# Memory attention: values with the weight as the moving operand, keys with both memory parts in one pass, and an 8-column product in two passes

## The chip, the cores and the metric

One core of a Trainium2 chip runs the whole program. The metric is the device time of one execution in microseconds (us); shorter is better. The engines are TensorE (PE in the profile; its weight loads are PEld), VectorE (DVE), ScalarE (ACT), GpSimd (POOL) and SyncE (SP, which issues nearly all transfers).

## What is computed

The reference runs two transformer blocks in float32 on 512 tokens of 1024 channels. The second block has a gated delta-rule mixer, an attention from the 512 tokens to 256 memory tokens, and a feed-forward part. What the change touches, in the reference's own words:

```python
proj = hn @ w_in[l]                                   # 2568 columns; the last 8 are b (4) and a (4)
beta = jax.nn.sigmoid(b)
g = -jnp.exp(a_log) * jax.nn.softplus(a + dt_bias)
...
m = rmsnorm_2(mem, mem_norm_g[l])                     # 256 x 1024
q = (h @ w_q).reshape(B, S, 4, 256)                   # 512 tokens
k = (m @ w_k).reshape(B, M, 4, 256)                   # 256 memory tokens
v = (m @ w_v).reshape(B, M, 4, 256)
s = jnp.einsum('bshd,bmhd->bhsm', q, k) * 256 ** -0.5
o = jnp.einsum('bhsm,bmhd->bshd', jax.nn.softmax(s, axis=-1), v).reshape(B, S, D_MODEL)
return o @ w_o
```

## The kernel before

Activations lie transposed: 8 chunks of 128 channels (partitions) by 512 tokens. Every large product is taken in a reduced float32 format (fp32r) with each operand split into a high part (a ScalarE cast) and a low part (the rest, one VectorE subtraction). `mm3` (line 224) makes three matmuls from a pair of blocks: high x high, high x low, low x high. A `unit` (line 230) takes one weight tile of 128 partitions x 1024 elements, that is 8 blocks of 128 x 128, and makes 128 output channels with 8 x 3 matmuls into one PSUM bank; the weight is the stationary operand and the activations are the moving one, 512 columns, or 256 for the memory. The result is evacuated by VectorE and ScalarE with the norm's factor, then split again. A `group` (line 247) starts several units with their first `part` chunks and finishes the rest afterwards, so that TensorE has work while the last chunks of the input come in.

Weights come in the order of a plan (`unit_plan`, line 65) written out by hand. `w_dma` (line 165) loads a tile of 512 KB on SP's queue into one of two staging buffers "wst"; `w_split` (line 175) makes its high part "wh" on ScalarE (L187) and its low part "wl" on VectorE (L188), three buffers each. `w_prefetch` (line 191) splits up to two tiles and loads up to four ahead of the unit.

TensorE executes in the order of the program. The other engines' instructions are ordered when the program is built, by a priority: the place in the program, with evacuations, splits and loads of a unit raised by 400 places (`high_priority`). Background work is written as generators in a list; `tick` (line 206) lets each take one step after a unit, and so TensorE's instructions of such a step stand between two units.

The second mixer (`mix2`, line 1165) begins with a group of two units with `part` 6: the tile with the 8 gate columns (number 20 of `w_in_2`, the columns 0 to 3 and 32 to 35 of an otherwise empty tile) and unit 0. `gates` (line 864) transposes the gate rows and computes the decay on VectorE (L875 to L895); two small matmuls (L899, L900) use it. At its end the output projection runs 8 units of 4 blocks (`w_out_21`, line 1235), with `mem_prep` (line 1288) in the background: it loads the memory, splits it with its gain, sums its squares on GpSimd, and in its fifth step makes the norm of the memory's 256 tokens (`norm_R`, line 347: a matmul with ones into the PSUM tile "sm", which has one buffer at this point, then Ln, Exp and a correction step, L298 to L305).

The memory attention (`xa`, line 1315) runs the units of `XA_ORDER` (line 56): keys 0 to 2, then for each head two query units with keys between, then two value units. Keys and values are made transposed, 24 matmuls of 256 columns each. A value unit's result is scaled and, one tick later, turned by two transposes (L1331) and split into "xv". `xhead` (line 1246) is a head's attention in four steps: the scores of the 512 tokens and their softmax; an empty step; the transposes of the probabilities and their split; the product with the values, which overwrites the head's queries in "oh" and "ol". The output projection follows as a group of three units and five single units.

Of the kernel before, what the change touches and what calls it, by code (L numbers as in the profile page):

```python
# [9 lines left out]
F32 = mybir.dt.float32  # L10
F32R = mybir.dt.float32r
# [4 lines left out]
P = 128  # L16
S = 512
D = 1024
# [34 lines left out]

XA_ORDER = [("w_xk_2", m) for m in range(3)]
for _h in range(4):
    for _m in (2 * _h, 2 * _h + 1):
        XA_ORDER.append(("w_xq_2", _m))
        if 3 + _m < 8:  # L60
            XA_ORDER.append(("w_xk_2", 3 + _m))
    XA_ORDER += [("w_xv_2", 2 * _h), ("w_xv_2", 2 * _h + 1)]


def unit_plan():
# [40 lines left out]
class Kern:  # L106
# [68 lines left out]
    def w_split(self, i, parts=1):  # L175
        if i >= len(self.plan) or i in self.split_:
            return
        self.w_dma(i)
        nb = self.plan[i][2]
        st = self.staged[i]  # L180
        h = self.pw.tile([P, nb * P], F32R, tag="wh", name=self.nm("wh"), bufs=3)
        l = self.pw.tile([P, nb * P], F32R, tag="wl", name=self.nm("wl"), bufs=3)
        self.split_[i] = (h, l)
        n = nb * P // parts
        for p in range(parts):
            c = slice(p * n, p * n + n)
            r = self.nc.scalar.copy(h[:, c], st[:, c])  # L187
            self.nc.vector.tensor_tensor(out=l[:, c], in0=st[:, c], in1=h[:, c].bitcast(F32), op=ALU.subtract)  # L188
        return r
# [32 lines left out]


    def mm3(self, ps, h, l, xh, xl, first, last):
        mm = self.nc.tensor.matmul
        self.last_mm = mm(ps, h, xh, start=first, stop=False)  # L226
        mm(ps, h, xl, start=False, stop=False)  # L227
        mm(ps, l, xh, start=False, stop=last)  # L228

    def unit(self, name, idx, xs, evac, N=S, fill=0, mid=None, ps=None):  # L230
# [16 lines left out]
    def group(self, entries, xs, part, drain=False, fill=0):  # L247

        begun = []
        for i, (name, m, evac) in enumerate(entries):  # L250
            self.mark(f"{name}/{m}")
            wh, wl = self.w_get(name, m)
            ps = self.mm()
            begun.append((wh, wl, ps, evac))
            for k in range(part):
                sl = slice(k * P, k * P + P)
                self.mm3(ps[:], wh[:, sl], wl[:, sl], *xs[k], k == 0, False)
                if k == 0 and fill:
                    self.take(fill, self.last_mm)
            with self.tc.high_priority(offset=self.BOOST):  # L260
                self.w_prefetch(max(1, min(self.AHEAD_SPLIT, 2 - i)))
            if drain:
                self.tick()
        if drain:
            self.drain()
        for wh, wl, ps, evac in begun:
            for k in range(part, len(xs)):
                sl = slice(k * P, k * P + P)
                self.mm3(ps[:], wh[:, sl], wl[:, sl], *xs[k], False, k == len(xs) - 1)
            with self.tc.high_priority(offset=self.BOOST):  # L270
                self.w_prefetch()
                evac(ps)
            if not drain:
                self.tick()
# [589 lines left out]
    def gates(self, bar):  # L864
        nc = self.nc
        v, tt = nc.vector, nc.vector.tensor_tensor
        yield
        yield
        ps = self.sm()
        for n in range(4):  # L870
            nc.tensor.transpose(ps[:, n * P:(n + 1) * P], bar[:, n * P:(n + 1) * P], self.ccol("ident"))
        pv = ps[:].rearrange("p (n c) -> p n c", n=4)
        v4 = lambda t: t[:].rearrange("p (n h) -> p n h", n=4)
        beta, y, w, e, s2, p = (self.small(k) for k in ("beta", "gy", "gw", "ge", "gs2", "gp"))
        v.tensor_scalar(out=v4(beta), in0=pv[:, :, 0:4], scalar1=-1.0, scalar2=80.0, op0=ALU.mult, op1=ALU.min)  # L875
        tt(out=v4(y), in0=pv[:, :, 32:36], in1=self.vcol("dt_bias_2", 0, 16).rearrange("p (n h) -> p n h", n=4),
           op=ALU.add)
        v.scalar_tensor_tensor(out=w[:], in0=y[:], scalar=-1.0, in1=y[:], op0=ALU.mult, op1=ALU.max)
        nc.scalar.activation(e[:], w[:], AF.Exp, scale=-1.0)
        nc.scalar.activation(beta[:], beta[:], AF.Exp)  # L880
        v.tensor_scalar(out=beta[:], in0=beta[:], scalar1=1.0, scalar2=None, op0=ALU.add)
        v.reciprocal(beta[:], beta[:])
        v.tensor_scalar(out=w[:], in0=e[:], scalar1=2.0, scalar2=None, op0=ALU.add)
        v.reciprocal(w[:], w[:])
        tt(out=e[:], in0=e[:], in1=w[:], op=ALU.mult)
        tt(out=s2[:], in0=e[:], in1=e[:], op=ALU.mult)
        v.tensor_scalar(out=p[:], in0=s2[:], scalar1=1.0 / 17, scalar2=None, op0=ALU.mult)
# [12 lines left out]
        nc.tensor.matmul(ps[:, 16:32], self.ccol("gt"), g[:], start=True, stop=True)  # L900
        bg, kd = self.small("gbg"), self.small("gkd")
        nc.scalar.activation(bg[:], ps[:, 0:16], AF.Exp)
        nc.scalar.activation(kd[:], ps[:, 16:32], AF.Exp)
        tt(out=bg[:], in0=bg[:], in1=beta[:], op=ALU.mult)
        self.g_beta, self.g_g, self.g_bg, self.g_kd = beta, g, bg, kd
        self.g_last = self.small("glast")
# [381 lines left out]
    def mem_prep(self):  # L1288

        nc = self.nc  # L1290
        M = 256
        mem = self.big("mem", F32R)[:].rearrange("p c (h t) -> p h c t", h=2)
        macc, raw = self.pm.tile([P, M], F32, tag="msum", name="msum"), []
        for i in range(4):
            raw.append(self.c5("memr", 4)[:, :S].rearrange("p (k t) -> p k t", k=2))
# [1 line left out]
        for k in range(ND):  # L1297
# [6 lines left out]
                self.split(mem[:, 0, k, :], mem[:, 1, k, :], src, self.vcol("mem_norm_g_2", k))  # L1304
            if k % 2 == 1:
                yield
        ops = [(mem[:, 0, k, :], mem[:, 1, k, :]) for k in range(ND)]
        for _ in range(0):
            yield
        self.mem = ops, self.norm_R([macc[:]], N=M, after=self.last_sq)  # L1310

    last_mm = None
    mem = None
# [1 line left out]
    def xa(self, gnext):  # L1315
# [5 lines left out]
        if self.mem is None:  # L1321
            self.bg.append(self.mem_prep())
            self.drain()
        ms, RM = self.mem
        self.xk = self.pm.tile([P, 2, 8, M], F32R, tag="xk", name="xk")
        self.xv = self.pm.tile([P, 2, 2, D], F32R, tag="xv", name="xv")
        def v_tr(m, t):
            yield
            ps = self.pd()
            for mb in range(2):  # L1330
                nc.tensor.transpose(ps[:, mb * P:mb * P + P], t[:, mb * P:mb * P + P], self.ccol("ident"))  # L1331
            self.split(self.xv[:, 0, :, m * P:m * P + P], self.xv[:, 1, :, m * P:m * P + P],
                       ps[:, :M].rearrange("p (a c) -> p a c", a=2))
        getR = self.lazy_R(xacc)
        self.oh, self.ol = self.big("oh", F32R), self.big("ol", F32R)
        for name, m in XA_ORDER:
            def ev_k(ps):
                t = self.scaled(ps, RM, N=M)
                self.split(self.xk[:, 0, m, :], self.xk[:, 1, m, :], t[:, :M])

            def ev_q(ps):
                t = self.scaled(ps, getR())
                self.split(self.oh[:, m, :], self.ol[:, m, :], t[:])

            def ev_v(ps):
                self.bg.append(v_tr(m, self.scaled(ps, RM, N=M)))
            if name == "w_xq_2":
                self.unit(name, m, xs, ev_q)
            else:
                self.unit(name, m, ms, ev_k if name == "w_xk_2" else ev_v, N=M)  # L1350
            if name == "w_xv_2" and m % 2 == 0:
                self.bg.append(self.xhead(m // 2))
        self.reload_x()
        os_ = [(self.oh[:, k, :], self.ol[:, k, :]) for k in range(ND)]
        self.units("w_xo_2", ND, os_, self.FIRST_XO, 6,
# [152 lines left out]
def layout(inp):  # L1508
# [5 lines left out]
    for t in ("ffn1", "ffn2"):  # L1514
        a[t + "_wgu"] = tile_w(g[t + "_wgu"][0])
        for s, (lo, hi) in enumerate(((0, 8), (8, 16), (16, 22))):
            a[f"{t}_wdown{s}"] = tile_w(g[t + "_wdown"][0], lo * P, hi * P)
    for n in ("w_in", "attn_proj", "conv_proj", "w_out", "ple_proj", "ple_gate_w", "w_xk_2", "w_xv_2",
              "w_xq_2", "w_xo_2", "w_up_2"):
        a[n] = tile_w(g[n][0])  # L1520
    w = g["w_in_2"][0]
    pad = np.zeros((D, 21 * P), w.dtype)
    pad[:, :2560] = w[:, :2560]
# [41 lines left out]
```

## Time and profile before

| | |
|---|---|
| median of 3 runs | 2045.68 us (2045.57 to 2047.61) |
| the profiled execution | 2047.42 us |
| its span in the profile | 2045.6 us, 25091 instructions |
| TensorE busy | 2004.0 us (98%), 9564 matmuls |
| VectorE / ScalarE / GpSimd busy | 1218.2 / 881.0 / 237.5 us |
| mean granted TensorE clock | 0.994 of full speed |

The span runs from the first instruction to the last; the profiled execution's own time has 1.8 us more around it. A matmul's end in the profile is modelled, and consecutive matmuls overlap, so the price of one is read from start to start. In brackets behind an instruction stand the idle time of its engine before it and what ended that. Transfers and semaphore waits don't count as busy.

### The profile page before, as it was taken

How to read it: one execution, taken by the hardware profiler on the slowest of the kernel's cores; microseconds unless marked ns; L12 is line 12 of the kernel's file. 1: busy time of each engine (PE TensorE's matmuls, PEld its weight loads, DVE VectorE, ACT ScalarE, POOL GpSimd, SP SyncE). 2: the span in 40 equal slices, each digit the busy share in tenths (PEclk: the TensorE clock that was granted, in tenths of full speed). 3: DMA queues.
4: the chain of work that ended last, by engine and by line, in shares of the span. 5: the costliest groups of instructions: out<-in, count | busy, mean ns of one | idle time of the engine just before them, and what ended most of it. 6: DMA issues, size and time to landing. Idle time of an engine off the chain costs nothing. (4 is left out here: it accounts for less than half of the span.)

```text
span 2045.6 us, 25091 instructions
## 1 busy us (share of the span) xinstructions
PE 2004.0 (98%) x9564; PEld 1672.0 (82%) x9564; DVE 1218.2 (60%) x1956; ACT 881.0 (43%) x1467; POOL 237.5 (12%) x234
## 2 busy tenths in 40 slices
PE   8999999999998999999999999999999999999997
PEld 6888888787887888888888877888989888888886
DVE  6434445899889865543444577677576654344344
ACT  5223223665778544422222364463464444233233
POOL 0000000296224300000000012135000000000001
PEclk9999999999899999999999999999999999999999
DMA  5232323322221234232232234221044422232322
GB/s 181 94 103 93 102 94 105 127 93 95 69 72 60 68 124 154 93 100 96 96 100 93 85 101 137 93 78 53 17 155 129 139 83 93 94 102 93 100 96 73
DMA packets 65672, 201.13 MB, mean 98 GB/s; under 512 B 7312, under 2 KB 11536, under 8 KB 65424
## 3 DMA queue, kind: packets, MB, share of 16 engines
q1 hardware_dynamic: 64864, 199.00, 29.8%
q8 instruction: 76, 1.25, 0.2%
q10 hardware_dynamic: 688, 0.53, 0.1%
q14 instruction: 44, 0.36, 0.1%
HBM read 188.75 MB, written 10.49 MB: 97 GB/s over the span
## 5 line engine op out<-in xcount | busy, mean ns | idle before, releaser
L187 ACT CAST wh<-wst 128x1024 fp32r<-128x1024 f32 (+3 forms) x357 | 353.9, 993 | 892.4 <-PE mm L227 633.8
L226 PE MATMUL mm<-xh,wh 128*128 128x512 f32 x1272 | 502.6, 395 | 2.6 <-ACT xh L290 1.5
L228 PE MATMUL mm<-xh,wl 128*128 128x512 f32 x1272 | 496.1, 390 | 0.7 <-DVE wl L188 0.5
L227 PE MATMUL mm<-xl,wh 128*128 128x512 f32 x1272 | 495.5, 390 | 0.3 <-DVE xl L291 0.3
L188 DVE TENSOR_TENSOR wl<-wst,wh 128x1024 fp32r<-128x1024 f32 (+3 forms) x357 | 420.0, 1178 | 74.3 <-ACT wh L187 73.9
L226 PEld LDWEIGHTS mm<-xh,wh 128*128 128x128 f32 x1272 | 239.1, 188 | 55.4 <-issue 3.2
L227 PEld LDWEIGHTS mm<-xl,wh 128*128 128x128 f32 x1272 | 239.1, 188 | 52.7 <-issue 3.4
L228 PEld LDWEIGHTS mm<-xh,wl 128*128 128x128 f32 x1272 | 238.9, 188 | 51.4 <-DVE wl L188 1.5
L227 PE MATMUL mm<-hl,wh 128*128 128x512 f32 (+1 forms) x616 | 238.2, 387 | 0.2
L226 PE MATMUL mm<-hh,wh 128*128 128x512 f32 (+1 forms) x616 | 238.3, 387 | 0.0
L228 PE MATMUL mm<-hh,wl 128*128 128x512 f32 (+1 forms) x616 | 238.0, 386 | 0.0
L371 DVE SCALAR_TENSOR_TENSOR x<-mm,x 128x512 f32<-128x512 f32 x111 | 76.6, 690 | 249.7 <-PE mm L228 246.9
L651 POOL TENSOR_TENSOR y<-y,cv 128x512 f32<-128x512 f32 x90 | 131.8, 1464 | 126.0 <-ACT cv L650 109.1
L227 PEld LDWEIGHTS mm<-hl,wh 128*128 128x128 f32 x616 | 115.7, 188 | 24.3 <-DVE hl L288 1.0
L226 PEld LDWEIGHTS mm<-hh,wh 128*128 128x128 f32 x616 | 115.7, 188 | 23.6
L228 PEld LDWEIGHTS mm<-hh,wl 128*128 128x128 f32 x616 | 115.7, 188 | 23.3
L226 PE MATMUL mm<-xnh,wh 128*128 128x512 f32 x304 | 121.3, 399 | 0.7 <-DVE z L389 0.7
L228 PE MATMUL mm<-xnh,wl 128*128 128x512 f32 x304 | 119.6, 394 | 0.0
L227 PE MATMUL mm<-xnl,wh 128*128 128x512 f32 x304 | 119.5, 393 | 0.0
L438 DVE TENSOR_TENSOR t<-mm,R 128x512 f32<-128x512 f32 x43 | 29.7, 691 | 138.4 <-PE mm L228 138.3
L659 DVE SCALAR_TENSOR_TENSOR cacc<-u,vec,cacc 128x512 f32<-128x512 f32 x145 | 108.9, 751 | 2.8
L432 DVE TENSOR_TENSOR t<-mm,R 128x512 f32<-128x512 f32 x43 | 29.7, 691 | 94.1 <-PE mm L228 94.0
(406 smaller groups left out, 2829.0 us busy)
## 6 DMA issues: line engine op xcount, KB each, us to landing
wst<-ffn_wgu SPq DMA_DIRECT2D x86, 512.0 KB, 3.4
wst<-w_in SPq DMA_DIRECT2D x63, 512.0 KB, 3.4
wst<-ffn_wdown SPq DMA_DIRECT2D x32, 512.0 KB, 3.4
wst<-w_up SPq DMA_DIRECT2D x32, 512.0 KB, 3.4
wst<-w_down SPq DMA_DIRECT2D x32, 512.0 KB, 3.5
wst<-ffn_wdown SPq DMA_DIRECT2D x16, 384.0 KB, 3.0
xd<-x SPq DMA_DIRECT2D x24, 256.0 KB, 2.1
x<-xd SPq DMA_DIRECT2D x24, 256.0 KB, 5.2
```

The source lines that it names most:

```text
L187: r = self.nc.scalar.copy(h[:, c], st[:, c])
L188: self.nc.vector.tensor_tensor(out=l[:, c], in0=st[:, c], in1=h[:, c].bitcast(F32), op=ALU.subtract)
L226: self.last_mm = mm(ps, h, xh, start=first, stop=False)
L227: mm(ps, h, xl, start=False, stop=False)
L228: mm(ps, l, xh, start=False, stop=last)
L371: self.nc.vector.scalar_tensor_tensor(out=x, in0=ps[:], scalar=scale, in1=x, op0=ALU.mult, op1=ALU.add)
L432: nc.vector.tensor_tensor(out=t[:], in0=ps[:], in1=R[:], op=ALU.mult)
L438: nc.vector.tensor_tensor(out=t[:], in0=ps[:], in1=R[:], op=ALU.mult)
L651: eng.tensor_tensor(out=y, in0=y, in1=t[:], op=ALU.add)
L659: yield eng.scalar_tensor_tensor(out=y if j == 29 else acc, in0=u[:, j:j + S], scalar=w(j), in1=acc, op0=ALU.mult, op1=ALU.add)
```

## The change

- **Values.** The weight `w_xv_2` is laid out by rows: tile k holds rows 128 k to 128 k + 127 with all 1024 columns, 512 KB as before. A value unit now takes chunk k of the normalised memory as the stationary operand (two blocks of 128 tokens) and the weight tile as the moving one (two halves of 512 columns), 4 x 3 matmuls of 512 columns, into four PSUM banks ("pd") that collect all eight units. The result has the memory tokens on partitions, as "xv" wants it, so the transposes are gone; the norm's factor is now one per partition.
- **That factor** is made in `mem_prep`: two matmuls of one column into "sm", one VectorE operation that reads them, and a small reciprocal root; the norm over the columns for the keys (`norm_R`) follows it.
- **Keys.** The memory's high and low parts lie side by side (2 x 256 columns), and the high weight takes both in one matmul of 512 columns; the low weight takes the high part in one of 256. The evacuation adds the two halves: a ScalarE copy and a VectorE addition are new.
- **Order.** All eight value units come first, then keys 0 and 1, then queries and keys in turn; a head's attention is appended after its second query unit.
- **The 8 gate columns.** The weight tile keeps its high part in columns 0 to 63 and its low part in 64 to 127 of one stationary tile, so that `mm3` makes two matmuls, not three; `gates` adds the two parts after its transposes.

```diff
-XA_ORDER = [("w_xk_2", m) for m in range(3)]
-for _h in range(4):
-    for _m in (2 * _h, 2 * _h + 1):
-        XA_ORDER.append(("w_xq_2", _m))
-        if 3 + _m < 8:
-            XA_ORDER.append(("w_xk_2", 3 + _m))
-    XA_ORDER += [("w_xv_2", 2 * _h), ("w_xv_2", 2 * _h + 1)]
+XA_ORDER = [("w_xv_2", m) for m in range(8)] + [("w_xk_2", m) for m in range(2)]
+for _m, _k in enumerate((2, 3, 4, 5, None, 6, None, 7)):
+    XA_ORDER.append(("w_xq_2", _m))
+    if _k:
+        XA_ORDER.append(("w_xk_2", _k))
+NARROW = ("w_in_2", 20)
...
     def w_split(self, i, parts=1):
         h = self.pw.tile([P, nb * P], F32R, tag="wh", name=self.nm("wh"), bufs=3)
+        if self.plan[i][:2] == NARROW:
+            h3, s3 = (t[:].rearrange("p (k c) -> p k c", c=P) for t in (h, st))
+            r = self.nc.scalar.copy(h3[:, :, :64], s3[:, :, :64])
+            self.nc.vector.tensor_tensor(out=h3[:, :, 64:], in0=s3[:, :, :64], in1=h3[:, :, :64].bitcast(F32),
+                                         op=ALU.subtract)
+            self.split_[i] = (h, None)
+            return r
...
     def mm3(self, ps, h, l, xh, xl, first, last):
         self.last_mm = mm(ps, h, xh, start=first, stop=False)
-        mm(ps, h, xl, start=False, stop=False)
+        mm(ps, h, xl, start=False, stop=last and l is None)
+        if l is None:
+            return
         mm(ps, l, xh, start=False, stop=last)
...
     def gates(self, bar):
-        v.tensor_scalar(out=v4(beta), in0=pv[:, :, 0:4], scalar1=-1.0, scalar2=80.0, op0=ALU.mult, op1=ALU.min)
-        tt(out=v4(y), in0=pv[:, :, 32:36], in1=self.vcol("dt_bias_2", 0, 16).rearrange("p (n h) -> p n h", n=4),
-           op=ALU.add)
+        nc.scalar.copy(v4(w), pv[:, :, 64:68])
+        nc.scalar.copy(v4(e), pv[:, :, 96:100])
+        tt(out=v4(beta), in0=pv[:, :, 0:4], in1=v4(w), op=ALU.add)
+        tt(out=v4(y), in0=pv[:, :, 32:36], in1=v4(e), op=ALU.add)
+        v.tensor_scalar(out=beta[:], in0=beta[:], scalar1=-1.0, scalar2=80.0, op0=ALU.mult, op1=ALU.min)
+        tt(out=y[:], in0=y[:], in1=self.vcol("dt_bias_2", 0, 16), op=ALU.add)
...
     def mem_prep(self):
-        ops = [(mem[:, 0, k, :], mem[:, 1, k, :]) for k in range(ND)]
-        self.mem = ops, self.norm_R([macc[:]], N=M, after=self.last_sq)
+        ps, v = self.sm(), self.small("mv", 2)
+        rc = self.pt.tile([P, 2], F32, tag="rmc", name="rmc")
+        for mb in range(2):
+            nc.tensor.matmul(ps[:, mb:mb + 1], macc[:, mb * P:mb * P + P], self.ccol("ones", 0, 1),
+                             start=True, stop=True)
+        nc.vector.tensor_scalar(out=v[:], in0=ps[:, :2], scalar1=1.0 / D, scalar2=EPS, op0=ALU.mult, op1=ALU.add)
+        self.rsqrt_small(v[:], rc[:], "mr")
+        self.mem = both, self.norm_R([macc[:]], N=M, after=self.last_sq), rc
...
     def xa(self, gnext):
+        def v_unit(k):
+            wh, wl = self.w_get("w_xv_2", k)
+            for i in range(4):
+                mb, cs = i // 2, slice(i % 2 * H, i % 2 * H + H)
+                ts = slice(mb * P, mb * P + P)
+                self.mm3(vps[i][:], mem[:, 0, k, ts], mem[:, 1, k, ts], wh[:, cs], wl[:, cs], k == 0, k == ND - 1)
+            with self.tc.high_priority(offset=self.BOOST):
+                self.w_prefetch()
+                if k == ND - 1:
+                    for i in range(4):
+                        at = slice(None), i // 2, slice(i % 2 * H, i % 2 * H + H)
+                        self.split(self.xv[:, 0][at], self.xv[:, 1][at], vps[i][:], RMc[:, i // 2:i // 2 + 1])
+            self.tick()
+        def k_unit(m):
+            wh, wl = self.w_get("w_xk_2", m)
+            ps = self.mm()
+            for k in range(ND):
+                sl = slice(k * P, k * P + P)
+                nc.tensor.matmul(ps[:], wh[:, sl], both[:, k, :], start=k == 0, stop=False)
+                nc.tensor.matmul(ps[:, :M], wl[:, sl], mem[:, 0, k, :], start=False, stop=k == ND - 1)
+            with self.tc.high_priority(offset=self.BOOST):
+                self.w_prefetch()
+                t = self.t2("z")
+                nc.scalar.copy(t[:, M:], ps[:, M:])
+                nc.vector.tensor_tensor(out=t[:, :M], in0=ps[:, :M], in1=t[:, M:], op=ALU.add)
+                nc.vector.tensor_tensor(out=t[:, :M], in0=t[:, :M], in1=RM[:, :M], op=ALU.mult)
+                self.split(self.xk[:, 0, m, :], self.xk[:, 1, m, :], t[:, :M])
+            self.tick()
+        vps = [self.pd() for _ in range(4)]
...
-            if name == "w_xv_2" and m % 2 == 0:
-                self.bg.append(self.xhead(m // 2))
+            if name == "w_xv_2":
+                v_unit(m)
+            elif name == "w_xk_2":
+                k_unit(m)
+            else:
+                self.unit(name, m, xs, ev_q)
+                if m % 2:
+                    self.bg.append(self.xhead(m // 2))
...
+    a["w_xv_2"] = np.ascontiguousarray(g["w_xv_2"][0].reshape(ND, P, D))
```

## Rows read from the trace of the kernel before

**Rows 1.** The page's busy time, share of the span and instructions by engine

```profile
PE 2004.0 (98%) x9564; PEld 1672.0 (82%) x9564; DVE 1218.2 (60%) x1956; ACT 881.0 (43%) x1467; POOL 237.5 (12%) x234
```

**Rows 2.** Timeline of TensorE, 1503 to 1521 us: start, duration, line, operands (us)

```profile
1503.58 0.39 PE L226 MATMUL mm<-yd,wh 128*128 128x512 f32 x1
...
1508.79 0.39 PE L228 MATMUL mm<-yd,wl 128*128 128x512 f32 x1
...
1518.00 0.28 PE L226 MATMUL mm<-mem,wh 128*128 128x256 f32 x1
...
1520.64 0.28 PE L227 MATMUL mm<-mem,wh 128*128 128x256 f32 x1
```

**Rows 3.** Timeline of TensorE at a pair of value transposes

```profile
1551.06 0.38 PE L1331 MATMUL pd<-cst,z 128*128 128x128 f32 x2
1551.19 0.36 PE L226 MATMUL pd<-xk,oh 128*128 128x256 f32 x1
1551.39 0.28 PE L227 MATMUL pd<-xk,oh 128*128 128x256 f32 x1
```

**Rows 4.** Timeline of TensorE at the start of the second mixer

```profile
1258.25 0.50 PE L226 MATMUL mm<-xh,wh 128*128 128x512 f32 x1 [1.48 <-ACT xh L290]
...
1259.38 0.63 PE L228 MATMUL mm<-xh,wl 128*128 128x512 f32 x1
1259.81 1.91 PE L350 MATMUL sm<-ss,cst 128*128 128x512 f32 x2
```

**Rows 5.** Busy time by stretch; after the five engines the granted clock, DMA share, GB/s

```profile
1258.20:1260.00 1.80, 1.47 (x4) 1.00 (x5) 0.78 (x2) 1.62 (x2) 0.00 (x0) 0.82 0.89 246
1260.00:1262.50 2.50, 2.50 (x6) 1.27 (x5) 1.22 (x1) 1.39 (x2) 0.00 (x0) 0.50 0.37 141
```

**Rows 6.** Timeline of VectorE, the gate chain

```profile
1272.49 0.16 DVE L876 TENSOR_TENSOR gy<-sm,vec 128x16 f32<-128x16 f32 x1
...
1279.25 1.01 DVE L895 SCALAR_TENSOR_TENSOR gg<-gy,ge 128x16 f32<-128x16 f32 x1
```

**Rows 7.** Timeline of TensorE, the small matmuls of the gates

```profile
1281.24 0.29 PE L899 MATMUL sm<-gg,cst 128*128 128x16 f32 x2
...
1281.61 1.10 PE L1162 MATMUL pd<-pp,wpool 128*128 128x512 f32 x2
```

**Rows 8.** Timeline of TensorE, the start of the memory attention

```profile
1521.59 0.39 PE L228 MATMUL mm<-mem,wl 128*128 128x256 f32 x1 [0.67 <-DVE wl L188]
...
1527.52 0.40 PE L227 MATMUL mm<-xl,wh 128*128 128x512 f32 x1
1528.07 0.50 PE L228 MATMUL mm<-xh,wl 128*128 128x512 f32 x1
```

**Rows 9.** Timeline of TensorE, the memory's norm

```profile
1509.02 0.59 PE L350 MATMUL sm<-msum,cst 128*128 128x256 f32 x2
```

**Rows 10.** Timeline of VectorE behind the memory's norm

```profile
1509.72 0.68 DVE L188 TENSOR_TENSOR wl<-wst,wh 128x512 fp32r<-128x512 f32 x1
...
1513.67 0.69 DVE L188 TENSOR_TENSOR wl<-wst,wh 128x512 fp32r<-128x512 f32 x1
...
1514.87 0.41 DVE L301 TENSOR_SCALAR rv<-sm 128x256 f32<-128x256 f32 x1
```

**Rows 11.** Timeline of VectorE, low parts of three weight tiles

```profile
1516.33 1.23 DVE L188 TENSOR_TENSOR wl<-wst,wh 128x1024 fp32r<-128x1024 f32 x1 [0.45 <-ACT wh L187]
...
1520.32 1.22 DVE L188 TENSOR_TENSOR wl<-wst,wh 128x1024 fp32r<-128x1024 f32 x1
...
1539.29 1.22 DVE L188 TENSOR_TENSOR wl<-wst,wh 128x1024 fp32r<-128x1024 f32 x1 [0.66 <-ACT wh L187]
```

**Rows 12.** Timeline of VectorE, evacuation of a query unit

```profile
1559.82 0.69 DVE L389 TENSOR_TENSOR z<-mm,R 128x512 f32<-128x512 f32 x1 [1.72 <-PE mm L228]
...
1561.86 0.68 DVE L288 TENSOR_TENSOR ol<-z,oh 128x512 fp32r<-128x512 f32 x1
```

**Rows 13.** Busy time by stretch, in the scans of the second mixer

```profile
1400.00:1440.00 40.00, 39.77 (x364) 39.56 (x365) 22.92 (x88) 17.27 (x59) 10.67 (x22) 1.00 0.03 8
```

More of the change, by code (lines that the diff above doesn't have):

```diff
@@ L256, in group @@
                 sl = slice(k * P, k * P + P)
-                self.mm3(ps[:], wh[:, sl], wl[:, sl], *xs[k], k == 0, False)
+                self.mm3(ps[:], wh[:, sl], wl and wl[:, sl], *xs[k], k == 0, False)
                 if k == 0 and fill:
@@ L268, in group @@
                 sl = slice(k * P, k * P + P)
-                self.mm3(ps[:], wh[:, sl], wl[:, sl], *xs[k], False, k == len(xs) - 1)
+                self.mm3(ps[:], wh[:, sl], wl and wl[:, sl], *xs[k], False, k == len(xs) - 1)
             with self.tc.high_priority(offset=self.BOOST):
@@ L1291, in mem_prep @@
         M = 256
-        mem = self.big("mem", F32R)[:].rearrange("p c (h t) -> p h c t", h=2)
+        both = self.big("mem", F32R)
+        mem = both[:].rearrange("p c (h t) -> p h c t", h=2)
         macc, raw = self.pm.tile([P, M], F32, tag="msum", name="msum"), []
@@ L1306, in mem_prep @@
                 yield
-        ops = [(mem[:, 0, k, :], mem[:, 1, k, :]) for k in range(ND)]
-        for _ in range(0):
-            yield
-        self.mem = ops, self.norm_R([macc[:]], N=M, after=self.last_sq)
+        ps, v = self.sm(), self.small("mv", 2)
[6 more added lines that the diff above has]
+        self.mem = both, self.norm_R([macc[:]], N=M, after=self.last_sq), rc
     last_mm = None
@@ L1323, in xa @@
             self.drain()
-        ms, RM = self.mem
+        both, RM, RMc = self.mem
+        mem = both[:].rearrange("p c (h t) -> p h c t", h=2)
         self.xk = self.pm.tile([P, 2, 8, M], F32R, tag="xk", name="xk")
         self.xv = self.pm.tile([P, 2, 2, D], F32R, tag="xv", name="xv")
[L1327 to L1333, printed above, removed]
+        H = D // 2
+        def v_unit(k):
[27 more added lines that the diff above has]
+        vps = [self.pd() for _ in range(4)]
         getR = self.lazy_R(xacc)
@@ L1336, in xa @@
         for name, m in XA_ORDER:
-            def ev_k(ps):
-                t = self.scaled(ps, RM, N=M)
-                self.split(self.xk[:, 0, m, :], self.xk[:, 1, m, :], t[:, :M])
             def ev_q(ps):
@@ L1343, in ev_q @@
                 self.split(self.oh[:, m, :], self.ol[:, m, :], t[:])
-            def ev_v(ps):
-                self.bg.append(v_tr(m, self.scaled(ps, RM, N=M)))
-            if name == "w_xq_2":
+            if name == "w_xv_2":
[3 more added lines that the diff above has]
+            else:
                 self.unit(name, m, xs, ev_q)
-            else:
-                self.unit(name, m, ms, ev_k if name == "w_xk_2" else ev_v, N=M)
-            if name == "w_xv_2" and m % 2 == 0:
-                self.bg.append(self.xhead(m // 2))
+                if m % 2:
+                    self.bg.append(self.xhead(m // 2))
         self.reload_x()
@@ L1517, in layout @@
             a[f"{t}_wdown{s}"] = tile_w(g[t + "_wdown"][0], lo * P, hi * P)
-    for n in ("w_in", "attn_proj", "conv_proj", "w_out", "ple_proj", "ple_gate_w", "w_xk_2", "w_xv_2",
-              "w_xq_2", "w_xo_2", "w_up_2"):
+    for n in ("w_in", "attn_proj", "conv_proj", "w_out", "ple_proj", "ple_gate_w", "w_xk_2", "w_xq_2",
+              "w_xo_2", "w_up_2"):
         a[n] = tile_w(g[n][0])
+    a["w_xv_2"] = np.ascontiguousarray(g["w_xv_2"][0].reshape(ND, P, D))
     w = g["w_in_2"][0]
```

## The prediction

> **What bounds the kernel now.** I read the page's busy times first: TensorE is busy for nearly the whole span [rows 1], so the question is TensorE's own order of work, and every other engine matters only where TensorE waits for it. Next I read the timeline of TensorE for the price of a matmul, start to start. From 1503.58 to 1508.79 us there are 23 steps of 512 columns, 5.21 / 23 = 0.2265 us each, and from 1518.00 to 1520.64 us 22 steps of 256 columns, 2.64 / 22 = 0.120 us each [rows 2]. At 2.4 GHz, the upper level, 512 and 256 columns are 0.2133 and 0.1067 us; what is left over is 0.013 us in both. So a column costs one cycle and a matmul 0.013 us on top. Third, I looked for waits around the two places of the change: the start of the second mixer and the end of it, where the memory attention begins.
>
> **The change part by part.** The values' product had 8 units x 24 matmuls of 256 columns = 192 and gets 8 x 12 = 96 of 512. The columns are the same, so 96 x 0.0133 = 1.28 us go. The keys had 192 of 256 and get 64 of 512 and 64 of 256: again the same columns, 64 matmuls fewer, 0.85 us. Together **-2.13 us**, all on TensorE's path. The Trainium skill, "TensorE: Matmul & The Clock Gate", section "Back-to-back issue gap", gives N / 2.4 + 2.5 ns for a warm matmul; by that the 160 matmuls would be worth an estimated 0.4 us and the sum below would be 1.7 us higher, but the rows here show 13 ns.
>
> The 16 transposes of the values leave with the old order. A pair starts at 1551.06, the matmul behind it at 1551.19 and the next at 1551.39 [rows 3]: 0.13 us, and 0.08 more because that gap is 0.20 instead of 0.12. That is 0.21 to 0.22 us a pair, eight pairs, **-1.76 us**.
>
> The projection of the 8 gate columns loses 8 of its 24 matmuls, on paper 8 x 0.2265 = 1.81 us. But it stands first in the second mixer, and TensorE waits there: after 6 + 6 + 1 blocks of three matmuls it stands idle until 1258.25 for the last chunk of the normalised input [rows 4], and that chunk comes from the chain of the gate stage before it, which the change doesn't touch. Seven of the eight removed matmuls stand ahead of this wait and only make it longer. One stands behind it, the row at 1259.38, whose successor starts at 1259.81: **-0.43 us**. Bounds: -1.81, and +1 if the longer idle time keeps the clock at its lower level longer (the window after it was granted 0.82, then 0.50 [rows 5]). The split of that weight tile is half as long, off the path. The gate chain gains two ScalarE copies and two small VectorE operations. Its result is ready at 1279.25 + 1.01 = 1280.26 [rows 6] and TensorE uses it at 1281.24 [rows 7]: 0.98 us of cover, against some 0.5 to 0.9 us that I estimate for four small operations (the small VectorE row is 0.16 us [rows 6], handoffs are on top), with TensorE 0.4 us earlier. I take 0; with the cover gone it is up to 0.4 us.
>
> Two matmuls of one column give the memory's norm by rows. Their nearest rows are the two of 16 columns, 1281.24 to 1281.61 [rows 7]: **+0.37 us**.
>
> What waits at the old start of the memory attention may go: TensorE waited for the low part of a weight tile, 1520.64 to 1521.59 where 0.12 was due, and 1527.52 to 1528.07 where 0.23 was due [rows 2, 8]: 0.83 + 0.32 = **-1.15 us**, if nothing takes their place.
>
> **The added wait.** In the last step of the memory's preparation the two new matmuls write the PSUM tile "sm", of which there is one buffer, and the matmul of the norm right behind them takes the same buffer. It has to wait until VectorE has read the two columns, and TensorE's order is written by hand, so the units 5 to 7 of the output projection (lines 1234 to 1235) stand behind it. The read has no raised priority, while the evacuations and splits on VectorE have. In the profile the norm's matmul starts at 1509.02 [rows 9], and VectorE comes to that tile's reader (L301) only at 1514.87; eight operations, from the row at 1509.72 on, go ahead of it without a hole in VectorE's queue [rows 10]. With TensorE waiting, the last of those eight (an evacuation of unit 5) can't come, so the read would follow the operation at 1513.67, done near 1514.43, against 1509.02 + 0.37 = 1509.39 for the new matmuls: **+5.0 us**. Bounds: 0.2 us (the read is slotted in at once) and 5.5 us (it comes where L301 came). I take 5.0 because the nearest row is the same bank, at the same place, with the same queue ahead. So long an idle time also costs clock. After the wait at the second mixer [rows 4], 1.8 and 2.5 us were granted 0.82 and 0.50 [rows 5]: 1.8 x 0.18 + 2.5 x 0.50 = **+1.6 us**.
>
> **The weight tiles.** Ten units of about 2.75 us now stand in a row (12 x 0.2265 = 2.72, 8 x 0.3465 = 2.77), where the old order put a unit of 5.4 us after three. Low parts were ready at 1516.33 + 1.23 = 1517.56 for the first tile and 1539.29 + 1.22 = 1540.51 for the eighth [rows 11]: 22.95 / 7 = 3.28 us a tile, in a stretch where other work (a table load, the old keys' evacuations) held them up; I estimate 3.05 without it. Nine intervals are short by 9 x 0.3 = 2.7 us. But during the added wait SP, ScalarE and VectorE go on, up to three split and two staged tiles, so the values start with about one tile of lead: **+0.4 us**. Without that lead it is +3.0 us.
>
> The rest I cost at nothing. The values' evacuation is four ScalarE and four VectorE operations of 512 columns at the last value unit, the keys' one more on each engine; they replace eight and sixteen smaller ones, and VectorE is busy for only 60% of the span [rows 1]. If that cover fails, the four VectorE operations are 4 x 0.69 = 2.8 us of its queue. An odd query unit now has one key unit of 2.77 us between its end and the first head's scores, which need its low part 0.6 us after they begin, so 3.4 us; the row pattern is 1559.82 to 1561.86 + 0.68, some 2.9 us after the unit's end [rows 12]. That is cover of 0.5 us, and 0 to 0.5 us if it is late. For the later heads the next head's value product lies between. SP issues as many transfers of the same size as before.
>
> **Sum:** -2.13 - 1.76 - 0.43 + 0.37 - 1.15 + 5.0 + 1.6 + 0.4 = **+1.9 us**. The profiled execution took 2047.42 us (span 2045.6 us), 1.74 above the median of 2045.68 and at the upper end of the runs; the difference is put on the median: **2047.6 us**. A measurement of this kernel can tell about 0.2% from no change, 4.1 us.
>
> **The rivals.** (1) The read comes early. VectorE slots the two-column read between evacuations and TensorE hardly waits; then there is no lead, and the value units run at the pace of the tiles: -5.1 + 0.2 + 3.0 = -1.9 us, **2043.8**. For it: the read needs one small operation. Against it: a full queue [rows 10]. (2) The read comes early and the tiles keep up as well, at 2.75 us each: -4.9 us, **2040.8**, faster. Against it: no stretch of the trace shows tiles that fast. (3) The tiles decide. At the early pace of 3.28 us, the lead of one tile (2.7 us) is used up after five of the nine intervals, and the shortage is 9 x 0.53 - 2.7 = 2.1 us; with the first interval as slow as before (1517.56 to 1520.32 + 1.22 = 1521.54, 3.98 us) it is 1.2 more, 3.3 in place of the 0.4: about +4.8 us, **2050.5**, slower. Its place is the low part of the tiles on VectorE, and it decides from 9 x (pace - 2.75) > 2.7, a pace over 3.05 us. For it: [rows 8, 11]. (4) The values' units go round four PSUM banks. The scans of the second mixer, which change bank every four matmuls, ran at a granted 1.00 [rows 13], so I see no cost. At the lower level (1.2 GHz) a step is 0.43 us [rows 4], and 96 x 0.20 would add 19.5 us: **2067**. The Trainium skill, "TensorE: Matmul & The Clock Gate", section "A second HAM failure mode: psum-queue depth-cycling", tells of a kernel whose clock oscillated when it cycled through banks; the scans here don't agree.
>
> **How the numbers follow.** The forecast has 0.52, the rivals 0.24, 0.10, 0.12 and 0.02. The forecast and rival 1 lie within 0.2% but for their edges; rival 2 is faster; rivals 3 and 4 and a late read make it slower. Faster 0.13, the same 0.70, slower 0.17. The range runs from 2041.5 (leaving out rival 2) to 2051.0 (leaving out half of rival 3 and rival 4).
>
> **What would show it.** Right: in the timeline of TensorE, a gap of 4 to 5 us in the row of the norm's matmul (L350 on "msum"), with VectorE's read of the two columns as releaser and a granted clock near 0.5 behind it; value matmuls 0.2265 us apart; the wait at the start of the second mixer longer by about 1.6 us, still released by the input's last chunk. Wrong: no gap at that matmul, which is rival 1 or 2; then gaps of 0.3 us before each value unit, released by the tile's low part, tell 1 from 2. Gaps of that kind after a long wait are rival 3. A granted clock near 0.5 all through the value units is rival 4. Waits before the value products of heads two and three would be an edit that I cost at nothing.

## The result, and the profile after

| | before | after |
|---|---|---|
| median of the comparison | 2046.37 us (2045.57 to 2047.61) | 2089.83 us (2088.69 to 2093.52) |
| ratio, 95% interval | | 1.0214 (1.0201 to 1.0226) |
| the profiled execution, its span | 2047.42, 2045.6 us | 2089.96, 2088.2 us |

The forecast was 2047.6 us in a range of 2041.5 to 2051.0; the changed kernel is slower by some 43 us. The page of the kernel after, the row that answers to [rows 1]:

```profile
span 2088.2 us, 24733 instructions
...
PE 2044.5 (98%) x9384; PEld 1660.9 (80%) x9384; DVE 1216.5 (58%) x1958; ACT 884.4 (42%) x1475; POOL 237.3 (11%) x234
```

TensorE has 180 matmuls fewer than before and is busy for 40.5 us more. So the time is not a wait: the matmuls themselves take longer. Busy time by stretch of the kernel after, first in the first block, which the change does not touch, then around the memory's norm and in the value units (after the five engines the granted clock, the DMA share, GB/s):

```profile
200.00:240.00 40.00, 40.00 (x173) 32.22 (x172) 18.23 (x22) 11.44 (x14) 0.00 (x0) 1.00 0.28 96
1534.60:1539.70 5.10, 0.50 (x6) 0.41 (x4) 4.94 (x9) 4.33 (x7) 0.00 (x0) 0.90 0.79 240
1539.70:1545.40 5.70, 5.70 (x14) 4.46 (x15) 1.76 (x6) 1.68 (x5) 0.00 (x0) 0.50 0.35 110
1551.30:1573.40 22.10, 22.10 (x96) 17.77 (x95) 12.11 (x14) 11.46 (x13) 0.00 (x0) 1.00 0.59 186
```

In the first row 40.00 us hold 173 matmuls at a granted clock of 1.00. In the kernel before the same stretch holds 179:

```profile
200.00:240.00 40.00, 40.00 (x179) 33.12 (x178) 17.06 (x21) 11.06 (x14) 0.00 (x0) 1.00 0.32 105
```

The timeline of TensorE at the first value unit of the kernel after shows the step:

```profile
1551.26 0.39 PE L236 MATMUL pd<-wh,mem 128*128 128x512 f32 x1
...
1551.96 0.39 PE L236 MATMUL pd<-wh,mem 128*128 128x512 f32 x1
```

Three steps, from the first row to the second, take 0.70 us, 0.2333 us each, where [rows 2] show 0.2265. Over the whole trace the steps of 512 columns under 0.26 us average 226.9 ns before and 233.2 ns after, at the same mean granted clock (0.994 and 0.993). By the start of the second mixer [rows 4] the changed kernel is already some 23 us late.

What the prediction did speak of is there too. The start of the second mixer and the memory's norm, TensorE after (they answer to [rows 4, 9]):

```profile
1279.85 0.40 PE L237 MATMUL mm<-xl,wh 128*128 128x512 f32 x1
1281.77 0.49 PE L236 MATMUL mm<-xh,wh 128*128 128x512 f32 x1 [1.53 <-ACT xh L302]
...
1534.58 0.50 PE L1326 MATMUL sm<-cst,msum 128*128 128x1 f32 x4
1539.68 1.22 PE L362 MATMUL sm<-msum,cst 128*128 128x256 f32 x2 [4.60 <-DVE mv L1328]
```

And VectorE in that stretch, which answers to [rows 10]:

```profile
1538.88 0.68 DVE L197 TENSOR_TENSOR wl<-wst,wh 128x512 fp32r<-128x512 f32 x1
1539.48 0.15 DVE L1328 TENSOR_SCALAR mv<-sm 128x2 f32<-128x2 f32 x1
```

The matmul of the norm waits, released by the read of two columns, which comes right behind the low part of a weight tile, the last piece of the queue; the window behind it was granted 0.50.

### The profile page after: what moved, and what is told of

Its sections match the earlier page's. It is cut to its first block, busy times and chain, and to the rows that moved or that the text cites. A ratio compares the mean times of both kernels' runs of the same rounds, so it can differ in the third digit from the quotient of the medians.

```text
span 2088.2 us, 24733 instructions
## 1 busy us (share of the span) xinstructions
PE 2044.5 (98%) x9384; PEld 1660.9 (80%) x9384; DVE 1216.5 (58%) x1958; ACT 884.4 (42%) x1475; POOL 237.3 (11%) x234
## 5 line engine op out<-in xcount | busy, mean ns | idle before, releaser
L236 PE MATMUL mm<-xh,wh 128*128 128x512 f32 x1272 | 510.0, 401 | 2.6 <-ACT xh L302 1.5
L237 PE MATMUL mm<-xl,wh 128*128 128x512 f32 x1272 | 503.6, 396 | 0.3 <-DVE xl L303 0.3
L237 PEld LDWEIGHTS mm<-xl,wh 128*128 128x128 f32 x1272 | 239.2, 188 | 60.6 <-issue 3.4
```

Source lines behind the costliest of these rows:

```text
L237: mm(ps, h, xl, start=False, stop=last and l is None)
```

## The experiments

The change also adds one small thing that the prediction did not look at: the tile "rmc" for the values' factor, 2 columns, 32 bytes of each partition. In the built program it takes the place at address 127680, and all that lies behind it moves up by 32 bytes: the staging buffers, "wh" (135872 to 135904), "wl", and the tiles of the later phases. The activations lie below and stay. My first theory, for e1 to e4, was that a weight buffer off a multiple of 64 bytes makes each matmul slower; from e5 on it was that the move of the weights against the activations does. Rivals: the change's code, an extra instruction, or the absolute address.

**e1: the place alone.** The kernel before with an unused tile in that place; every address is as in the kernel after.

```diff
 macc, raw = self.pm.tile([P, M], F32, tag="msum", name="msum"), []
+self.nc.gpsimd.memset(self.pt.tile([P, 2], F32, tag="pad", name="pad")[:], 0.0)
```

> The kernel before with one unused tile of 2 columns (32 bytes a partition), cleared once on GpSimd, put where the changed kernel puts its new tile of factors: ahead of the weight buffers, which move from byte 135872 (a multiple of 64) to 135904 (not one) with everything behind them. Theory 'place': the step of a 512-column matmul goes from 226.6 to 233.3 ns in the whole program, as in the changed kernel, and the time to about 2089 us (ratio 1.021; 7.0 ns over some 6300 such matmuls is 42 us). Theory 'edits' (operand roles, order or instructions of the changed kernel make it slow): 2046 us, ratio 1.000, steps of 226.6 ns.

Measured: 2083.95 us, 1.018 of before (1.0167 to 1.0194), steps of 233.2 ns. That is 36.5 us of the 43.5, with none of the change's work.

```profile
200.00:240.00 40.00, 40.00 (x173) 32.17 (x173) 18.10 (x22) 11.46 (x14) 0.00 (x0) 1.00 0.27 93
```

The row is the stretch of 200 to 240 us of this kernel: 173 matmuls, clock 1.00, as after.

**e2: 64 bytes.** The changed kernel with that tile 16 columns wide, so that the weights stand at multiples of 64 bytes again.

```diff
-rc = self.pt.tile([P, 2], F32, tag="rmc", name="rmc")
+rc = self.pt.tile([P, 16], F32, tag="rmc", name="rmc")[:, :2]
```

> The changed kernel with the new tile of factors 16 columns wide instead of 2 (64 bytes), so that the weight buffers start at 135936, a multiple of 64 again. Theory 'place': steps of 226.6 ns and the sum of the forecast, 1.9 us over before plus 1.2 us for the wait before the last head's scores that the trace after shows, about 2049 us (2044 to 2051, ratio 0.999 to 1.002). Theory 'edits': 2089 us, ratio 1.021.

Measured: 2091.21 us, 1.0237 (1.0211 to 1.0264); steps of 233.3 ns. My theory had 2049 here and failed: a multiple of 64 is not what counts. Theory "edits" had the number right, but e1 has none of the edits. (The profiled execution took 2105.6 us, and one more of the six 2106.14. In its trace TensorE was granted 0.50 for 34 us of the second mixer's scans, from 1426.6 us on, where no other trace has more than 3.4 us at that level; why stays open. Only steps at full clock are read.)

One product does not fit the 233.3. In the value units of this run, where the weight tile is the moving operand, the 95 steps from the first row to the second take 21.76 us, 229.1 ns each:

```profile
1567.16 0.40 PE L236 MATMUL pd<-wh,mem 128*128 128x512 f32 x1
...
1588.92 0.39 PE L240 MATMUL pd<-wh,mem 128*128 128x512 f32 x1
```

**e3: the wait taken away.** As e2, with the two one-column matmuls in the PSUM ring "pd" of four buffers.

```diff
-ps, v = self.sm(), self.small("mv", 2)
+ps, v = self.pd(), self.small("mv", 2)
```

> As the run before, and the two matmuls of the row factor write a PSUM tile of the other kind (four buffers) instead of the single buffer of the norm. The trace after shows TensorE idle for 4.60 us at the norm's matmul and some 14 matmuls at the lower clock behind it. If that wait costs what the forecast said (5.0 + 1.6 us, less the lead in weight tiles that it gave, 2.6 us): about 4 us less than the run before, 2045 us. If the tiles keep up without the lead: 6.6 us less, 2042 us. If the wait was free because TensorE would have waited elsewhere: the same as the run before.

Measured: 2087.26 us, 1.0194 (1.018 to 1.0207), some 4 us less than e2 (3.5 without the two long executions of e2). The wait is worth what was expected, and is a tenth of the loss.

**e4: one operand of three.** The kernel before with the 32 bytes put between "wh" and "wl", so that "wh" keeps its address.

```diff
+if i == 0:
+    self.nc.gpsimd.memset(self.pw.tile([P, 2], F32, tag="pad", name="pad")[:], 0.0)
 l = self.pw.tile([P, nb * P], F32R, tag="wl", name=self.nm("wl"), bufs=3)
```

> The kernel before with the unused 2-column tile between the high and the low weight buffers: the high parts stay at 135872, the low parts (148160 to 148192) and the stage buffers behind move by 32 bytes. Theory 'place of the stationary operand, matmul by matmul': only matmuls with a low part as stationary operand take 233.3 ns, a third of them, about +14 us, 2060 us. Theory 'any of them off a multiple of 64 slows the whole stream': +42 us, 2089 us. Theory 'edits': 2046 us.

Measured: 2082.88 us, 1.0175 (1.0157 to 1.0193), 35.5 us more than before: near the second theory, though its 64 bytes are not what counts (e2). The three steps of a block now differ: high x high to high x low 232.2 ns, from there to low x high 239.2, from there to the next block 228.5 on average. Their sum, 699.9, is the same as with all three at 233.3. So moving one of the two weight parts costs the triple as much as moving both. And the cost does not stay with the matmul whose own operands were moved: the step of 232.2 lies between two matmuls whose operands all stand where they stood.

**e5: everything moved alike.** The kernel before with 32 unused bytes ahead of all tiles.

```diff
+self.nc.gpsimd.memset(self.pc.tile([P, 8], F32, tag="pad", name="pad")[:], 0.0)
 self.cst = self.pc.tile([P, NCST], F32, tag="cst", name="cst")
```

> The kernel before with an unused tile of 32 bytes allocated ahead of everything, so that every tile lies 32 bytes higher and no tile moves against another. Theory A (a matmul is slower where its moving and its stationary operand no longer stand at the same remainder of their addresses): nothing changes, steps of 0.2267 us for 512 columns and 2046 to 2048 us. Rival B (the absolute address of an operand counts): steps of 0.2333 us and about 2084 us, as when only the later tiles moved by 32 bytes. Rival C (the extra GpSimd instruction and tile do it, wherever they lie): about 2084 us too.

Measured: 2046.91 us, 1.000 (0.9991 to 1.0009), steps of 226.9 ns.

```profile
200.00:240.00 40.00, 40.00 (x178) 33.14 (x177) 17.03 (x20) 10.95 (x14) 0.00 (x0) 1.00 0.33 105
```

The stretch holds 178 matmuls at the same clock. The absolute address and the extra instruction are out: what counts is where the tiles stand against each other.

**e10, e11: how far.** As e1 with 128 bytes (the diff is against e1), and with 256, that is 64 columns.

```diff
-self.nc.gpsimd.memset(self.pt.tile([P, 2], F32, tag="pad", name="pad")[:], 0.0)
+self.nc.gpsimd.memset(self.pt.tile([P, 32], F32, tag="pad", name="pad")[:], 0.0)
```

> The kernel before with an unused tile of 128 bytes where the new tile of the change stands, so that the weight tiles move by 128 bytes against the activations. If only the remainder by 128 (or less) counts: 2046 to 2048 us and steps of 0.2267 us. If the remainder by 256 or 512 counts: about 2084 us and steps of 0.2333 us, as with 32 bytes.

> The kernel before with an unused tile of 256 bytes where the new tile of the change stands. If the remainder of the addresses by 256 counts: 2046 to 2048 us and steps of 0.2267 us. If the remainder by 512 counts: 2077 to 2085 us and steps of about 0.232 us, as with 128 bytes.

Measured: e10 2079.12 us, 1.0155 (1.0139 to 1.017), steps of 232.4 ns; e11 2046.05 us, 0.9998 (0.9988 to 1.0007), steps of 226.9 ns. The same stretch, of e10 and then of e11:

```profile
200.00:240.00 40.00, 40.00 (x174) 32.44 (x173) 18.23 (x22) 11.44 (x14) 0.00 (x0) 1.00 0.28 97
```

```profile
200.00:240.00 40.00, 40.00 (x178) 33.13 (x177) 17.49 (x21) 11.49 (x14) 0.00 (x0) 1.00 0.31 103
```

Moves of 32, 64 and 128 bytes cost; 256 doesn't, nor 512 (e12). The remainder by 256 fits all of them.

**e6 and e12: the change without the move.** In e6 the factor lies in bytes that were padding behind the table of constants:

```diff
-self.cst = self.pc.tile([P, NCST], F32, tag="cst", name="cst")
+self.cst = self.pc.tile([P, NCST + 2], F32, tag="cst", name="cst")
...
-rc = self.pt.tile([P, 2], F32, tag="rmc", name="rmc")
+rc = self.cst[:, NCST:]
```

In e12 its tile is padded to 512 bytes:

```diff
-rc = self.pt.tile([P, 2], F32, tag="rmc", name="rmc")
+rc = self.pt.tile([P, 128], F32, tag="rmc", name="rmc")[:, :2]
```

> The changed kernel with the factor kept in two columns appended to the table of constants, in bytes that were padding before, so that no tile moves against the kernel before. Theory A and rival B: steps of 0.2267 us again, and the time is that of the change's own terms: 2047 to 2049 us (the forecast of 2047.6 plus the 1.2 us wait of the last head's scores for key 7). Rival C or any other cause that lies in the change's code: still about 2089 us. The value units, whose stationary operand now stands at 0, 512, 1024 or 1536 bytes against the moving one, tell whether such distances cost anything: 0.2267 us a step if not.

> The changed kernel with its new tile padded to 512 bytes, so that the tiles behind it move by 512 bytes and keep their remainder by 512 against the activations. Theory (the distance of the operands by 512 or a divisor of it counts, since a weight block of 128 columns is 512 bytes long and all blocks cost the same): steps of 0.2267 us and the time of the kernel with the factor in the table of constants, 2050 to 2052 us. Rival (any move of the weights against the activations costs): about 2090 us.

Measured: e6 2050.95 us, 1.0018 (1.0009 to 1.0027); e12 2051.69 us, 1.0023 (1.0013 to 1.0032). Some 39 us are back, and what is left is the change itself. e6 lies 2 us above the 2047 to 2049 that I expected, but the kernel before ran at 2047.59 in that comparison, not at the 2045.68 I had started from: 3.1 us more than before was expected, 3.4 measured. Windows of e6, around the wait and in the value units:

```profile
1508.00:1515.00 7.00, 1.93 (x10) 1.58 (x9) 6.11 (x14) 4.69 (x8) 0.00 (x0) 0.78 0.68 193
1515.00:1525.00 10.00, 10.00 (x38) 8.09 (x37) 6.45 (x10) 5.81 (x9) 0.00 (x0) 0.81 0.40 142
1525.00:1550.00 25.00, 25.00 (x116) 20.84 (x115) 14.88 (x17) 14.27 (x16) 0.00 (x0) 1.00 0.57 183
```

TensorE's timeline of e6 at the memory's norm and at the scores of the last head:

```profile
1508.35 0.50 PE L1326 MATMUL sm<-cst,msum 128*128 128x1 f32 x4
1513.92 1.22 PE L362 MATMUL sm<-msum,cst 128*128 128x256 f32 x2 [5.07 <-DVE mv L1328]
...
1633.40 0.28 PE L240 MATMUL pd<-xk,ol 128*128 128x256 f32 x1
1634.57 0.38 PE L236 MATMUL pd<-xk,oh 128*128 128x256 f32 x1 [0.89 <-ACT xk L299]
```

Two waits stand in it: 5.07 us for the read, as forecast, and 0.89 us for key 7 at the last head's scores.

**e7: the wait gone as well.** e6 with the edit of e3.

> As the kernel with the factor in the table of constants, and the two one-column matmuls write a PSUM tile of the ring of four instead of the single one. Theory: the wait of 4.6 us at the norm's matmul and the half clock behind it go, some 4 to 6 us less than that kernel: 2042 to 2045 us, with up to 3 us given back if the values' tiles then come late. Rival (the wait only moves, to the read of the next user of the ring or to the tiles): within 1 us of that kernel.

Measured: 2047.95 us, 1.0003 (0.9994 to 1.0011): 3.0 less than e6, not 4 to 6; part is given back, as the expectation allowed. The norm's matmul no longer waits, but the values now do. TensorE and VectorE of e7:

```profile
1526.42 0.40 PE L236 MATMUL pd<-wh,mem 128*128 128x512 f32 x1
1527.54 0.50 PE L237 MATMUL pd<-wl,mem 128*128 128x512 f32 x1 [0.72 <-DVE wl L197]
```

```profile
1526.26 1.23 DVE L197 TENSOR_TENSOR wl<-wst,wh 128x1024 fp32r<-128x1024 f32 x1 [1.03 <-ACT wh L196]
...
1540.73 1.23 DVE L197 TENSOR_TENSOR wl<-wst,wh 128x1024 fp32r<-128x1024 f32 x1 [1.51 <-ACT wh L196]
```

Five intervals of low parts take 14.47 us, 2.89 each, against a unit of 2.72; VectorE itself waits, for ScalarE's high part, so what is late lies ahead of it. The chain of work that ended last, as the profile gives it for e7 (start, duration, what), shows what:

```profile
1528.98 1.24 DVE wl L197
...
1530.23 3.39 DMA wst<-w_xv
...
1533.72 1.06 ACT wh L196
...
1534.81 1.24 DVE wl L197
...
1536.06 3.49 DMA wst<-w_xk
```

ScalarE's cast of the tile between:

```profile
1531.04 1.05 ACT L196 CAST wh<-wst 128x1024 fp32r<-128x1024 f32 x1 [2.09 <-DMA wst<-w_xv]
```

A tile's transfer starts when the low part of an earlier tile has been made and a staging buffer is free; then the cast waits for the transfer, and the low part for the cast. From transfer to transfer that is 5.83 us here, for two staging buffers, so 2.9 us a tile. The cast itself does not hold things up: ScalarE stands idle for 1.6 to 2.1 us before it, until the transfer lands. No run tried a third staging buffer. The values and two keys take 30.1 us in e7 and 27.4 in e6.

**e8: the gate columns alone** on the kernel before (the diff is the change's own, parts `w_split`, `mm3` and `gates`).

> The kernel before with the edit of the 8 gate columns alone; no tile moves. My term: -0.4 us, the wait for the last chunk of the input longer by about 1.6 us and one matmul fewer behind it. Rival (the wait is not set by the input, so the removed matmuls count in full): -1.8 us. Rival (the longer idle time keeps the clock down longer, or the gate chain with its four more operations comes late): +0.4 to +1.4 us.

Measured: 2047.69 us, 1.000 (0.9991 to 1.0009). -1.8 is at the very edge of that interval, and -0.4 can't be told from nothing in the time. The steps in the trace can. TensorE of e8:

```profile
1254.61 0.39 PE L238 MATMUL mm<-xl,wh 128*128 128x512 f32 x1
1257.88 0.51 PE L237 MATMUL mm<-xh,wh 128*128 128x512 f32 x1 [2.88 <-ACT xh L303]
```

The step ahead of the last chunk's first matmul grew from 1.87 us (1256.38 to 1258.25) to 3.27, and from that matmul to the norm's there are 1.12 us in place of 1.56.

**e9: a lead for the tiles.** e7 with query 0 behind the second value unit; each of the keys 2 to 5 then comes behind a query that it stood ahead of. (Key 6 stands ahead of query 6 in e7 already.)

```diff
-XA_ORDER = [("w_xv_2", m) for m in range(8)] + [("w_xk_2", m) for m in range(2)]
+XA_ORDER = [("w_xv_2", 0), ("w_xv_2", 1), ("w_xq_2", 0)] + [("w_xv_2", m) for m in range(2, 8)]
+XA_ORDER += [("w_xk_2", 0), ("w_xk_2", 1), ("w_xq_2", 1)]
...
```

> As the kernel with the factor in the table of constants and the two matmuls into the ring of four, and query unit 0 stands behind the second value unit, key 6 ahead of query 6. Theory: in that kernel the value units wait about 2.7 us in sum for the low parts of their tiles, since eight short units stand in a row with no lead; a unit of 5.4 us among them gives the tiles a lead of 2.7 us, so 2 to 3 us less: about 2045 us. Rival (the query unit then waits itself for the last chunk of its input or its norm, or the tiles' pace is set by their transfers however the units stand): 2047 to 2048 us.

Measured: 2045.79 us, 0.9994 of before (0.9985 to 1.0003). The median is 2.2 us below that of e7, but the kernel before was 1.1 us faster in this comparison as well, and the two intervals overlap. So the time alone does not show a gain. The traces do: from the first product with the memory to the output projection e7 takes 116.64 us and e9 114.34, 2.3 less, as the theory had it, and no value unit from 1530.9 to 1547.2 us waits:

```profile
1530.90:1547.20 16.30, 16.30 (x73) 13.48 (x72) 9.38 (x10) 7.62 (x10) 0.00 (x0) 1.00 0.48 163
```

It is the best of the family, and still not to be told from the kernel before.

## Why the prediction was wrong

**The step that failed** is "The rest I cost at nothing". The 32-byte tile was in the diff, and no price was put on it. It costs about 39 us: e6, the change with the factor elsewhere and no tile moved, has a span of 2049.1 us against 2088.2. The steps of 512 columns below 0.26 us account for it: 7667 of 226.9 ns there, 1739.9 us, and 7673 of 233.2 ns after, 1789.0 us, +49; waits and steps of other sizes give 10 of that back (the longer steps of 512 columns, -7; those of 256 columns, -2; the rest, -1). Part of the -7 is a stretch of 6.8 us at a granted 0.50, from 511.8 us on, which e6 and the kernel before have and the slower kernel has not. That addresses move could have been seen from the diff. For the price the trace of before held one hint, which I didn't read: the 48 steps of the probabilities' product with the values average 232.7 ns there, where the others take 226.9.

**The other steps**, by e6, where nothing is moved, against before:

| stretch (first matmul to first matmul) | before | e6 | difference | forecast |
|---|---|---|---|---|
| the memory's norm to the first product with the memory | 8.63 | 16.54 | +7.91 | +0.37 + 5.0 + 1.6 = +6.97 |
| from there to the attention's output projection | 116.13 | 112.66 | -3.47 | -2.13 - 1.76 - 1.15 + 0.4 = -4.64 |

- **The added wait** was right in place, releaser and queue: the read came behind the low part of the weight tile, 5.4 us after the small matmuls started, and eight steps near 0.426 us and two longer ones followed. (By its row the operation ahead of the read was to end at 1514.36, not 1514.43 us; the term is 5.0 by either.) The term was 0.9 us too small. Without it (e7) the stretch takes 9.05 us, so the two small matmuls cost 0.41; the forecast was 0.37.
- **Values and keys.** 96 value steps of 0.2267 us, 21.76, stand against 192 that took 23.08: -1.32 (forecast -1.28). A key's pair of matmuls takes 0.3498 us where three took 0.3586, steps over 0.2 us left out of the three: 64 x 0.0088 = -0.56 (forecast -0.85). The pair was forecast at 0.3465: its matmul of 512 columns takes 0.2333 us with one of 256 behind it. The Trainium skill's 2.5 ns a matmul ("TensorE: Matmul & The Clock Gate", section "Back-to-back issue gap") would have given an estimated 0.4 us together; the runs give 1.88.
- **The transposes and the old waits** are gone as written; one of the eight pairs stood behind the stretch of the table, so -1.5 of the -1.76 falls in it.
- **A wait that I cost at nothing**: the scores of the last head wait for key 7, a step of 1.17 us where 0.12 is due, +1.05. I had looked at the query's low part ahead of head 0; the late one is the key behind the last query, with a longer evacuation. Added up by kind of step, the stretch's -3.47 is: products with the memory -2.92, queries -0.75, scores +1.19, value transposes -0.96, the rest -0.03. The old waits of the forecast stand in the first two, with a slower step right behind each, 0.22 us together, that it didn't count; behind the wait for key 7 there is a second long step among the scores, +0.37.
- **The tiles.** With the wait in place they had their lead, and cost nothing in e6 (forecast +0.4). Without it they cost about 2.7 us (e7), as rival 1 had it with 3.0; in e9 the lead of a query unit takes most of that away. In e7 another 1.1 us goes into two waits behind them: one for an evacuation (a step of 0.87 at 1562.29) and one of the first head's scores for the query's low part (0.59 at 1566.54), which is the wait that I had looked at.
- **The gate columns** behaved as argued (e8). One matmul behind the wait is gone, and the wait took up the other seven, but for 0.2 us. In the changed kernel itself the wait is 1.53 us, hardly longer than the 1.48 before, and so the sign that I had named is missing there: the 209 slower matmuls ahead of it in its group take 1.3 us of the idle time. With nothing moved (e6) it is 2.88.
- **Rival 4** falls: the value units change bank every three matmuls, and ran at a granted 1.00 in e6, e7 and e9. The oscillation of which the Trainium skill tells ("TensorE: Matmul & The Clock Gate", section "A second HAM failure mode: psum-queue depth-cycling") does not show in them. That the scans run at 1.00, my reason against this rival, holds for the whole of the second mixer's scans in all traces but those of e2 (34 us at 0.50) and e3 (3.4 us).

In sum the terms stand at +3.4 us by e6 (2050.95 against 2047.59; its interval is +1.8 to +5.5) where +1.9 was forecast. So the argument was about right for a change that moves no tile. Its misses there (the wait 0.9 too small, key 7 not counted, the products' gain 0.25 too large, the tiles 0.4 too dear) cancel in part, and that is luck. The change as written moves every tile behind the new one.

## What to carry to other kernels

A new tile is an edit of the address map, too: compare the addresses of the large operands before and after, and pad a small tile, or put it where nothing lies behind it, so that weights and activations keep their distance by a multiple of 256 bytes, the smallest of the moves tried that cost nothing. When a kernel gets slower, read the price of one matmul in a stretch that the edit doesn't touch before you look for waits. And when a wait is taken away, look at what it had given a lead.

## What the runs showed of the hardware

In these kernels the steps between fp32r matmuls of 512 columns averaged 226.9 ns where the addresses of a matmul's moving and stationary operands, within a partition, differed by a multiple of 256 bytes (e5, e6, e11, e12). They averaged 232.4 to 233.3 ns where the weights, as the stationary operand, had been moved against the activations by 32, 64 or 128 (e1, e2, e10), at the same granted clock. The value units bear it out within one kernel: in e6 their stationary block stands 0, 512, 1024 or 1536 bytes off by the same remainder, and all steps are 0.2267. So does a product that the change left alone: the probabilities ("pth", "ptl") and the values "xv" stand 128 off by 256 in the kernel before too, and those are the 48 steps of 232.7 ns.

Three readings show that this is not yet a rule for a single matmul. In e4 a step between two matmuls with unmoved operands takes 232.2 ns. In the value units, where the weights are the moving operand, the move by 32 costs as much as elsewhere (233.3 ns in the kernel after), but the move by 64 only 2 ns (229.1 in e2). And the keys' matmul of 512 columns, with one of 256 behind it, takes 233.3 ns in e6 with nothing moved. The products with 256 columns don't lose: the memory's steps under 0.2 us average 119.7 ns before and 118.5 in e1. In e1, e2, e4 and e10 the staging buffers move with the weights; that they are not the cause is argued from the probabilities' product alone, which has no staging buffer.

The Trainium skill, "SBUF — State Buffer", section "Operand start alignment", asks that an operand start at a multiple of its element size, and says that the rule is about legality, not speed; all addresses here satisfy it, and it does not speak of the 6 ns a matmul. Why the distance costs time isn't shown: the runs here only move addresses. Other data types, other distances and other numbers of columns weren't tried.
